# The scan of a two-block kernel: its small triangular solve on POOL, one scaling on ACT, and another order of the work in each step

## The chip, the cores and the metric

The kernel runs on one core of one Trainium2 chip. The metric is the device time of one execution in microseconds. The engines are PE (TensorE: matrix products), DVE (VectorE: elementwise work), ACT (ScalarE: functions and copies), POOL (GpSimd) and SP, which here only issues DMAs. Each takes its own queue in order; they wait for each other by semaphores.

## The reference

Two model blocks run one after the other on 512 tokens of width 1024, with 256 context tokens beside them. The first block has two layers. Each layer projects the tokens, runs a convolution over half of the channels and a recurrent scan over the other half, and then a gated feed-forward network. The second block has attention, retention and a mixture of 32 experts. The change touches the recurrent scan of the first block alone:

```python
def step(s, inp):                       # s: state, 64 x 64 for each of 8 heads
    r_t, k_t, v_t, w_t, kk_t, b_t = inp
    sa = -einsum("bhvk,bhk->bhv", s, kk_t)
    s = s * w_t[:, :, None, :] + sa[..., None] * b_t[:, :, None, :] + v_t[..., None] * k_t[:, :, None, :]
    y = einsum("bhvk,bhk->bhv", s, r_t) if emit else None
    return s, y
```

It runs forwards and backwards over the tokens, first over the 256 context tokens and then, from the state reached there, over the 512 tokens of x, in each of the two layers. Everything is float32.

## The kernel before

The scan of a layer is cut into 12 steps: four pairs of heads (a pair fills the 128 partitions), and for each pair three groups of 256 tokens. A step handles one group forwards and one backwards (the two entries of T), each as four chunks of 64 tokens. Within a chunk the recurrence becomes matrix products of 64x64 with the inverse of a triangular matrix I + N, which does not depend on the state. So for each step s these pieces of work are prepared ahead of the chunks:

- decays(s): the decay factors of all tokens (L842 to L876), with a memset on POOL at L860. Its two buffers tA and tB come from a ring of four, so that one step's decays can live at a time.
- products(s) (L878 to L913): scaled keys and queries (L886 to L892, on DVE), and their products on PE (L904), masked on DVE into GM (L908). One part of GM is N. For every third step norm_kk (L725) normalises the keys of a new pair first, through a buffer that the finish of an earlier pair also uses.
- solve(s) (L674 to L695): the inverse of the 16x16 blocks on the diagonal of I + N. N goes out to DRAM with four DMAs on SP (L682), and comes back as NB with one block to each of 64 partitions (L684). There 14 steps of substitution run, each one multiplication (L689) and one addition (L690) with k rows of 15 - k elements; the diagonal is set at L693, and the result goes out to DRAM (L694). NB is one buffer, the products' DRAM copies are two in turn.
- inverse(s): four DMAs on SP bring the blocks' inverses back in the layout of N (L702, in solved). DVE transposes them (L948), and by products on PE with copies on ACT and DVE between them (L954 to L1003) the 16x16 blocks grow to the whole 64x64 inverse XI. Beside it the keys are transposed on PE (L924).
- chunks(s) (L1009 to L1065): for each of four chunks the chain psR (PE, L1021 and L1024), rg (DVE, L1027), psS (PE, L1031), Z (ACT, L1033), psM (PE, L1039) and the new state M (DVE, L1044). M[:, 1] is the old state scaled by the decay of the chunk; L1043 writes it on POOL, and L1044 adds the new part.

The order is written out by generators. `abreast` takes one yield of each generator in turn; `among` runs the chunks of step s as the main work of 25 positions and spreads over them 16 yields of `to_come(s)` and 14 of `others(s)` (convolution taps at L533, gates of later layers with their weight loads at L250, the finish of an earlier pair). `to_come(s)` takes three yields of the inverse of s + 1 and then the rest of it abreast with products, solve and the following decays of s + 2. The Tile framework then plans the order on every engine from this: an instruction that comes earlier as written has priority, and one that its cost model takes to be ready may be moved ahead of one that is not.

Of the kernel before, what the change touches and what calls it, by code (L numbers as in the profile page):

```python
# [16 lines left out]
AF = mybir.ActivationFunctionType  # L17
OP = mybir.AluOpType
# [110 lines left out]
def tile_two_blocks(ctx: ExitStack, tc: tile.TileContext, I: dict, out: bass.AP, dump=None, stop=None):  # L129
    nc = tc.nc  # L130
# [51 lines left out]
    ones = const.tile([128, 128], F32, name="ones")  # L182
# [491 lines left out]
    def solve(s, T, gs):  # L674

        for q, (d, _) in zip(T, gs):
            src = q["NT"]
            if d:
                src = wk.tile([128, 4, 64], F32, name="Nt", tag="ar", bufs=1)
                nc.vector.transpose(src, q["NT"])  # L680
            for h in range(2):
                nc.sync.dma_start(own(NSC[s % 2], d, h), src[HR[h]])  # L682
        NB = wk.tile([64, 16, 16], F32, name="NB", tag="nb", bufs=1)
        nc.sync.dma_start(NB, blocks(NSC[s % 2]))  # L684
        yield
        for k in range(1, 15):
            t = wk.tile([64, 64], F32, name="nbt", tag="nbt", bufs=1)[:, 0:k * (15 - k)].rearrange("p (a b) -> p a b", a=k)
            sh = [64, k, 15 - k]
            nc.vector.tensor_tensor(t, NB[:, 0:k, k:k + 1].to_broadcast(sh), NB[:, k:k + 1, k + 1:16].to_broadcast(sh), op=OP.mult)  # L689
            nc.vector.tensor_tensor(NB[:, 0:k, k + 1:16], NB[:, 0:k, k + 1:16], t, op=OP.add)  # L690
            if k % 2:
                yield
        nc.vector.tensor_scalar(NB.rearrange("p a b -> p (a b)")[:, 0:256:17], ones[0:64, 0:16], 1.0, None, op0=OP.mult)  # L693
        nc.sync.dma_start(blocks(XSC[s % 2]), NB)  # L694
        yield  # L695

# [7 lines left out]
    def scan(l, S):  # L704
        RK, VY, WA = S["RK"], S["VY"], S["WA"]
        xd = dr.tile([128, KT * TT], F32, name=f"xd{l}")
        nc.sync.dma_start(xd, XT.rearrange("p a b -> p (a b)"))

        rkd = dr.tile([128, 2, 2, TT], F32, name=f"rkd{l}")
        wr = (TX if l == 1 else TT, TT)  # L710
        for i, w in enumerate(wr):
            nc.sync.dma_start(rkd[:, i, :, 0:w], RK[:, i, 2:4, 0:w])
        get = scan_buffers(l == 0, RK)
        w = TT if l == 0 else TX

        mods = [(0, u) for u in range(4, 12)] if l == 0 else []
        ZZ = [wk.tile([128, TT], F32, name=f"zz{i}", tag="z", bufs=zb[0]) for i in range(3)]
        S["rs"], S["V"] = ZZ[2], {}
        KKs, Ts, states = {}, {}, [[None, None] for _ in range(4)]

        def norm_kk(pr):

            KK = ZZ[pr % 2]
            for (a, n), p in zip(SEG, spread_halves(S["RN"][:, pr], 6, "pp", ZZ[2])):
                nc.vector.scalar_tensor_tensor(KK[:, a:a + n], RK[:, 1, pr % 2, a:a + n], vc("k_k", 4 * l + pr), p, op0=OP.mult, op1=OP.mult)  # L725
            KKs[pr] = KK

        def parts(s):
            pr, step = s // 3, s % 3
            return pr, step, [(0, step), (1, (0, 2, 1)[step])], not (l == 1 and step == 0)  # L730

        def decays(s):
            pr, step, gs, emit = parts(s)
            Ts[s] = [{}, {}]
            yield from abreast(decay(q, l, S, pr, d, g) for q, (d, g) in zip(Ts[s], gs))

        def every(f, s):
            pr, step, gs, emit = parts(s)
            yield from abreast(f(q, l, S, pr, d, g, KKs[pr], get, emit) for q, (d, g) in zip(Ts[s], gs))

        def blocks_of(s):
            if s % 3 == 0:
                norm_kk(s // 3)
                yield
            yield from every(products, s)
            yield from solve(s, Ts[s], parts(s)[2])

        def inverse_of(s):
            solved(s, Ts[s], parts(s)[2], get)
            yield from every(transposed, s)  # L750
            yield from inverse(Ts[s], parts(s)[2])

        def blocks_then_decays(s):
            yield from blocks_of(s)
            if s + 1 < 12:
                yield from decays(s + 1)

        def to_come(s):

            works = []  # L760
            if s + 1 < 12:
                works.append(inverse_of(s + 1))
                for _ in range(3):
                    yield next(works[0])
            if s + 2 < 12:
                works.append(blocks_then_decays(s + 2))
            yield from abreast(works)

        wcs = {}

        def conv_out(m):

            if m % 2 == 0 or not wcs:
                wcs[m // 2] = load_w(I["w_out"][l], 0, 4, (m // 2) * 256, 256)
            o = XT[:, m]
            if m < AHEAD_M:
                o = wk.tile([128, TT], F32, name="xm", tag="acc", bufs=1)
                nc.sync.dma_start(o[:, 0:w], xd[:, m * TT:m * TT + w])
            for i, (a, n) in enumerate(SEG[:1] if l == 1 else SEG):
                p = bank("pg", None, "pco")  # L780
                for kt in range(4):
                    nc.tensor.matmul(p[:, 0:n], lhsT=wcs[m // 2][:, kt, m % 2 * 128:m % 2 * 128 + 128], rhs=S["CV"][kt][:, a:a + n], start=kt == 0, stop=kt == 3)
                yield
                gated(o[:, a:a + n], p[:, 0:n], S["MOD"][:, i, 16 + m:17 + m], l == 1 and a < TX)
            if m < AHEAD_M:
                nc.sync.dma_start(xd[:, m * TT:m * TT + w], o[:, 0:w])
            yield

        def others(s):
            for f in S["conv"].get(s, ()):  # L790
                yield from f(S["rs"]) or ()
                yield
            for i, u in mods[s * len(mods) // ADA_STEPS:(s + 1) * len(mods) // ADA_STEPS]:
                ada(i, u)
                yield
            if s >= CONV_OUT:
                for m in range((s - CONV_OUT) * AHEAD_M // (12 - CONV_OUT), (s + 1 - CONV_OUT) * AHEAD_M // (12 - CONV_OUT)):
                    yield from conv_out(m)
            if s % 3 == 0 and s:
                yield from finish(l, S, s // 3 - 1)  # L800
                if s // 3 < 3:
                    for i, w in enumerate(wr):
                        nc.gpsimd.dma_start(RK[:, i, s // 3 - 1, 0:w], rkd[:, i, s // 3 - 1, 0:w])


        run(decays(0))
        run(blocks_of(0))
        run(decays(1))
        run(inverse_of(0))
        run(blocks_of(1))  # L810
        run(decays(2))
        for s in range(12):
            pr, step, gs, emit = parts(s)
            among(chunks(l, S, pr, gs, Ts[s], states[pr], emit, step == 2, get), MAIN, (to_come(s), AHEAD), (others(s), OTHERS[s]))
        for m in (*range(AHEAD_M, KT), *range(AHEAD_M)):
            nc.sync.dma_start(XT[:, m, 0:w], xd[:, m * TT:m * TT + w])
        run(abreast([finish(l, S, 3), chain(*(conv_out(m) for m in range(AHEAD_M, KT)))]))
# [7 lines left out]
    def run(work):  # L825
        for _ in work:
            pass
# [181 lines left out]
    def chunks(l, S, pr, gs, T, state, emit, final, get):  # L1009
# [4 lines left out]
        def chunk(q, d, n):  # L1014
            po = py[:, d] if emit else None
            c = n if d == 0 else 3 - n
            KR, GM, Z, BT, XI, PC = (q[k] for k in ("KR", "GM", "Z", "BT", "XI", "PC"))
            M = state[d]
# [16 lines left out]
            if not (final and n == 3):  # L1035
                pm = bank("sm", None, "psM")
                for i in range(2):
                    for h in range(2):
                        nc.tensor.matmul(pm[HR[h], 0:64], lhsT=BT[HR[h], c, i], rhs=Z[i][HR[h], c], start=i == 0, stop=i == 1)  # L1039
                yield  # L1040
                Mn = get("Mn").rearrange("p (a v) -> p a v", a=2)
                if M is not None:
                    nc.gpsimd.tensor_scalar(M[:, 1], M[:, 0], PC[:, c:c + 1], None, op0=OP.mult)  # L1043
                    nc.vector.scalar_tensor_tensor(Mn[:, 0], pm[:, 0:64], PC[:, c:c + 1], M[:, 1], op0=OP.mult, op1=OP.add)  # L1044
                else:
                    nc.vector.tensor_scalar(Mn[:, 0], pm[:, 0:64], PC[:, c:c + 1], None, op0=OP.mult)
                state[d] = Mn
# [310 lines left out]
    for t in range(6):  # L1358
        p = bank("pre", None, "rvt")
# [63 lines left out]
    for t in range(4):  # L1423
        for a, n in SEG:
            p = bank("pre", None, "pq")
# [8 lines left out]
    p = bank("w", None, "ppe")  # L1434
# [9 lines left out]
    for t in range(6):  # L1444
        r = LAT[:, 4 + t:5 + t]
        for i in range(2):
            p = bank("pre", None, "pkv")
# [19 lines left out]
    for t in range(6):  # L1467
        rk = SS[:, 4 + t]
        k, kp = KTL[t], KP[:, t:t + 1]
# [747 lines left out]
```

## Time and profile before

| | us |
|---|---|
| median of three runs | 4015.07 (4010.14 to 4015.51) |
| the profiled execution | 4013.53 |
| its span, first to last instruction | 4011.7 |
| PE busy in the span | 3774.9 |
| DVE busy | 2731.7 |
| ACT busy | 1695.0 |
| POOL busy | 333.9 |
| L689 and L690 together, DVE | 125.3 |
| L1043, POOL | 84.8 |

A stretch of the profile is read as the busy time of each engine in it; where two engines work at once, both are counted. In the lists of groups a row has the line, the engine, the operation, what it writes and reads by the program's names, its shape and its count, then its busy time and the mean duration of one, and then how long the engine stood idle just before such instructions, and for whom. A tile of the scan's buffers is shown as XT or scanbuf, since these buffers are cut from them. Starts are microseconds from the first instruction. The first scan lies at 289 to 691 us, the second at 1519 to 1869 us.

### The profile page before, as it was taken

The numbers are of one execution on the slowest core, as the hardware profiler recorded it, in microseconds if no ns is written. First come the engines' busy times: TensorE is split into PE (matmuls) and PEld (weight loads), VectorE is DVE, ScalarE is ACT, GpSimd is POOL, SyncE is SP. The second block draws the span as 40 slices with busy tenths as digits, with TensorE's granted clock in tenths as the row PEclk, the third lists the DMA queues.
The fourth block names the chain that finished last, engine by engine and source line by source line (L and its number), as shares of the span: only waits on it lengthen the run. The fifth ranks groups of instructions, "written<-read, shape, count | busy, mean of one in ns | idle before, by whom it ended". The sixth has DMA issues, their size and how long they took to land. (4 is left out here: it accounts for less than half of the span.)

```text
span 4011.7 us, 69029 instructions
## 1 busy us (share of the span) xinstructions
PE 3774.9 (94%) x27579; PEld 2827.9 (70%) x27579; DVE 2731.7 (68%) x5439; ACT 1695.0 (42%) x2530; POOL 333.9 (8%) x349
## 2 busy tenths in 40 slices
PE   6998999999999998999999998996999999999997
PEld 4787777888888786776787786675565777664443
DVE  4779865843433778876744545657877899987776
ACT  3233342321212334452322334544655677666555
POOL 0001111000000001110000000001101122122111
PEclk7999999999999998899999998997999999999999
DMA  6122323332322321124445421035979899998996
GB/s 204 47 79 69 115 71 98 117 123 84 126 84 85 100 72 25 32 45 125 152 151 153 106 74 42 1 117 198 360 279 351 306 363 363 371 354 331 374 368 240
DMA packets 353911, 677.75 MB, mean 169 GB/s; under 512 B 118759, under 2 KB 230194, under 8 KB 323474
## 3 DMA queue, kind: packets, MB, share of 16 engines
q1 hardware_dynamic: 343024, 636.89, 45.3%
q0 software_dynamic: 9312, 34.56, 3.4%
q8 instruction: 218, 3.57, 0.4%
q10 hardware_dynamic: 1250, 1.85, 0.1%
q14 instruction: 107, 0.88, 0.1%
HBM read 635.33 MB, written 37.90 MB: 168 GB/s over the span
## 5 line engine op out<-in xcount | busy, mean ns | idle before, releaser
L431 ACT ACTIVATE wh<-wst 128x1024 fp32r<-128x1024 f32 (+2 forms) x222 | 222.7, 1004 | 990.7 <-PE pc L441 513.1
L1830 DVE TENSOR_TENSOR ml<-E,mh 128x2048 fp32r<-128x2048 f32 x236 | 536.2, 2286 | 91.5 <-PE pu L1878 44.3
L1829 ACT ACTIVATE mh<-E 128x2048 fp32r<-128x2048 f32 x236 | 447.6, 1916 | 185.9 <-PE pu L1878 146.8
L441 PE MATMUL px<-Hh,wl 128*128 128x512 f32 (+2 forms) x1216 | 487.8, 402 | 13.8 <-DVE wl L432 13.8
L441 PE MATMUL px<-Hh,wh 128*128 128x512 f32 (+3 forms) x1216 | 486.1, 401 | 13.3 <-ACT wh L431 7.1
L441 PE MATMUL px<-Hl,wh 128*128 128x512 f32 (+3 forms) x1216 | 485.5, 400 | 0.6 <-DVE Hl L419 0.6
L432 DVE TENSOR_TENSOR wl<-wst,wh 128x1024 fp32r<-128x1024 f32 (+2 forms) x222 | 255.4, 1151 | 270.6 <-ACT wh L431 268.4
L1878 PE MATMUL pu<-ml,ch 128*64 128x512 f32 (+2 forms) x968 | 272.3, 399 | 22.4 <-DVE ml L1830 22.2
L1878 PE MATMUL pu<-mh,ch 128*128 128x512 f32 (+1 forms) x968 | 279.3, 403 | 6.9 <-DVE ch L1866 4.2
L441 PEld LDWEIGHTS px<-Hh,wh 128*128 128x128 f32 (+1 forms) x1216 | 232.2, 191 | 72.6 <-ACT wh L431 9.4
L441 PEld LDWEIGHTS px<-Hh,wl 128*128 128x128 f32 (+1 forms) x1216 | 231.8, 191 | 72.8 <-DVE wl L432 18.7
L441 PEld LDWEIGHTS px<-Hl,wh 128*128 128x128 f32 (+1 forms) x1216 | 232.4, 191 | 55.6 <-DVE Hl L419 3.5
L533 DVE SCALAR_TENSOR_TENSOR acc<-ZC,VT,acc 128x272 f32<-128x272 f32 (+2 forms) x600 | 253.0, 477 | 2.5 <-ACT acc L528 2.5
L1878 PEld LDWEIGHTS pu<-mh,ch 128*128 128x128 f32 (+1 forms) x968 | 171.8, 184 | 86.5 <-issue 25.0
L1830 DVE TENSOR_TENSOR ml<-st,mh 128x2048 fp32r<-128x2048 f32 x86 | 196.0, 2286 | 42.8 <-PE pu L1878 24.5
L1878 PEld LDWEIGHTS pu<-ml,ch 128*64 128x64 f32 (+2 forms) x968 | 149.4, 159 | 92.0 <-DVE ml L1830 34.1
L441 PE MATMUL pc<-Hh,wh 128*128 128x256 f32 x672 | 193.0, 288 | 1.0 <-ACT Hh L418 0.9
L441 PE MATMUL pc<-Hl,wh 128*128 128x256 f32 x672 | 191.9, 286 | 0.5 <-DVE Hl L419 0.5
L441 PE MATMUL pc<-Hh,wl 128*128 128x256 f32 (+1 forms) x672 | 190.3, 284 | 0.1
L1829 ACT ACTIVATE mh<-st 128x2048 fp32r<-128x2048 f32 x86 | 163.2, 1917 | 55.3 <-PE pu L1878 31.7
L315 DVE SCALAR_TENSOR_TENSOR as<-adt,CS,as 128x512 f32<-128x512 f32 x224 | 161.3, 747 | 36.4 <-DMA adt<-in_w_ada_dram 20.4
L1134 DVE SCALAR_TENSOR_TENSOR XT<-px,MOD,XT 128x512 f32<-128x512 f32 x66 | 49.4, 749 | 188.0 <-PE px L441 187.7
(602 smaller groups left out, 7864.2 us busy)
## 6 DMA issues: line engine op xcount, KB each, us to landing
E<-in_w_mlp_dram SPq DMA_DIRECT2D x288, 1024.0 KB
st<-in_w_mlp_dram SPq DMA_DIRECT2D x94, 1024.0 KB
wst<-in_w_in_dram SPq DMA_DIRECT2D x29, 1024.0 KB
adt<-in_ada_w_dram SPq DMA_DIRECT2D x96, 256.0 KB
adt<-in_w_ada_dram SPq DMA_DIRECT2D x96, 256.0 KB
wst<-in_ffn_wg_dram SPq DMA_DIRECT2D x22, 1024.0 KB
wst<-in_ffn_wu_dram SPq DMA_DIRECT2D x22, 1024.0 KB
adaw<-in_ada_w_dram SPq DMA_DIRECT2D x16, 1024.0 KB
```

Of the source, the lines that this page charges most:

```text
L315: nc.vector.scalar_tensor_tensor(acc[s], t, c, acc[s], op0=OP.mult, op1=OP.add)
L431: nc.scalar.activation(wh, t[:, :, c0:c0 + n], AF.Copy)
L432: nc.vector.tensor_tensor(wl, t[:, :, c0:c0 + n], f32(wh), op=OP.subtract)
L441: nc.tensor.matmul(p[0:m, 0:n], lhsT=wa[:, k, 0:m], rhs=ha[:, k, a:a + n], start=k == 0 and first, stop=k == nk - 1 and last)
L533: nc.vector.scalar_tensor_tensor(o, z[:, j + a:j + a + n], cw(j), o, op0=OP.mult, op1=OP.add)
L1134: nc.vector.scalar_tensor_tensor(o, src, gate, o, op0=OP.mult, op1=OP.add)
L1829: nc.scalar.activation(wh, t, AF.Copy)
L1830: nc.vector.tensor_tensor(wl, t, f32(wh), op=OP.subtract)
L1878: nc.tensor.matmul(p[0:xa.shape[2]], lhsT=xa[:, kt], rhs=w[part][:, c:c + 512], start=kt == 0 and j == 0, stop=last and j == len(parts) - 1)
```

## The change

The substitution of the solve is issued to POOL in place of DVE, with the diagonal. The scaling of the old state M goes from POOL to ACT. The old blocks_of is cut into products_of and solve_of. In `to_come(s)` the products of step s + 2 now stand first; then the solve of s + 2, followed by the decays of s + 3, runs abreast with the inverse of s + 1, the solve's generator first. Ahead of the steps, the products of step 1 are written before the inverse of step 0, and its solve behind it.

```diff
--- before.py
+++ after.py
@@ -686,11 +686,11 @@
         for k in range(1, 15):
             t = wk.tile([64, 64], F32, name="nbt", tag="nbt", bufs=1)[:, 0:k * (15 - k)].rearrange("p (a b) -> p a b", a=k)
             sh = [64, k, 15 - k]
-            nc.vector.tensor_tensor(t, NB[:, 0:k, k:k + 1].to_broadcast(sh), NB[:, k:k + 1, k + 1:16].to_broadcast(sh), op=OP.mult)
-            nc.vector.tensor_tensor(NB[:, 0:k, k + 1:16], NB[:, 0:k, k + 1:16], t, op=OP.add)
+            nc.gpsimd.tensor_tensor(t, NB[:, 0:k, k:k + 1].to_broadcast(sh), NB[:, k:k + 1, k + 1:16].to_broadcast(sh), op=OP.mult)
+            nc.gpsimd.tensor_tensor(NB[:, 0:k, k + 1:16], NB[:, 0:k, k + 1:16], t, op=OP.add)
             if k % 2:
                 yield
-        nc.vector.tensor_scalar(NB.rearrange("p a b -> p (a b)")[:, 0:256:17], ones[0:64, 0:16], 1.0, None, op0=OP.mult)
+        nc.gpsimd.tensor_scalar(NB.rearrange("p a b -> p (a b)")[:, 0:256:17], ones[0:64, 0:16], 1.0, None, op0=OP.mult)
         nc.sync.dma_start(blocks(XSC[s % 2]), NB)
         yield
 
@@ -738,11 +738,13 @@
             pr, step, gs, emit = parts(s)
             yield from abreast(f(q, l, S, pr, d, g, KKs[pr], get, emit) for q, (d, g) in zip(Ts[s], gs))
 
-        def blocks_of(s):
+        def products_of(s):
             if s % 3 == 0:
                 norm_kk(s // 3)
                 yield
             yield from every(products, s)
+
+        def solve_of(s):
             yield from solve(s, Ts[s], parts(s)[2])
 
         def inverse_of(s):
@@ -750,20 +752,20 @@
             yield from every(transposed, s)
             yield from inverse(Ts[s], parts(s)[2])
 
-        def blocks_then_decays(s):
-            yield from blocks_of(s)
+        def solve_then_decays(s):
+            yield from solve_of(s)
             if s + 1 < 12:
                 yield from decays(s + 1)
 
         def to_come(s):
 
+            if s + 2 < 12:
+                yield from products_of(s + 2)
             works = []
+            if s + 2 < 12:
+                works.append(solve_then_decays(s + 2))
             if s + 1 < 12:
                 works.append(inverse_of(s + 1))
-                for _ in range(3):
-                    yield next(works[0])
-            if s + 2 < 12:
-                works.append(blocks_then_decays(s + 2))
             yield from abreast(works)
 
         wcs = {}
@@ -804,10 +806,12 @@
 
 
         run(decays(0))
-        run(blocks_of(0))
+        run(products_of(0))
+        run(solve_of(0))
         run(decays(1))
+        run(products_of(1))
         run(inverse_of(0))
-        run(blocks_of(1))
+        run(solve_of(1))
         run(decays(2))
         for s in range(12):
             pr, step, gs, emit = parts(s)
@@ -1040,7 +1044,7 @@
                 yield
                 Mn = get("Mn").rearrange("p (a v) -> p a v", a=2)
                 if M is not None:
-                    nc.gpsimd.tensor_scalar(M[:, 1], M[:, 0], PC[:, c:c + 1], None, op0=OP.mult)
+                    nc.scalar.activation(M[:, 1], M[:, 0], AF.Copy, scale=PC[:, c:c + 1])
                     nc.vector.scalar_tensor_tensor(Mn[:, 0], pm[:, 0:64], PC[:, c:c + 1], M[:, 1], op0=OP.mult, op1=OP.add)
                 else:
                     nc.vector.tensor_scalar(Mn[:, 0], pm[:, 0:64], PC[:, c:c + 1], None, op0=OP.mult)
```

## Rows read from the trace of the kernel before

**Rows 1.** The page, part 1: busy us, share of the span, instructions of each engine

```profile
PE 3774.9 (94%) x27579; PEld 2827.9 (70%) x27579; DVE 2731.7 (68%) x5439; ACT 1695.0 (42%) x2530; POOL 333.9 (8%) x349
```

**Rows 2.** Busy time by stretch: its length, then PE, PEld, DVE, ACT, POOL busy (count)

```profile
345.00:500.00 155.00, 145.54 (x2886) 115.32 (x2886) 135.12 (x502) 56.39 (x158) 25.52 (x50) 0.97 0.38 110
500.00:691.00 191.00, 182.32 (x3301) 140.30 (x3300) 118.81 (x436) 73.65 (x186) 22.00 (x52) 0.98 0.30 77
1568.00:1700.00 132.00, 122.42 (x2530) 103.00 (x2532) 111.39 (x430) 51.01 (x146) 24.62 (x50) 0.87 0.16 31
1700.00:1869.00 169.00, 157.72 (x3023) 122.13 (x3020) 109.70 (x414) 72.41 (x184) 21.12 (x50) 0.96 0.26 62
```

**Rows 3.** Groups of instructions by line on DVE, whole span

```profile
L689 DVE TENSOR_TENSOR nbt<-NB 64x14 f32<-64x14 f32 (+6 forms) x336 | 62.8, 187 | 6.1 <-DMA NB<-nsc 3.2
...
L690 DVE TENSOR_TENSOR NB<-NB,nbt 64x14 f32<-64x14 f32 (+6 forms) x336 | 62.5, 186 | 2.5
```

**Rows 4.** DVE in order of time: first and last operations of solves

```profile
313.30 0.15 DVE L689 TENSOR_TENSOR nbt<-NB 64x14 f32<-64x14 f32 x1
...
328.01 0.17 DVE L690 TENSOR_TENSOR NB<-NB,nbt 64x14 f32<-64x14 f32 x1
...
642.02 0.17 DVE L689 TENSOR_TENSOR nbt<-NB 64x14 f32<-64x14 f32 x1
...
1537.58 0.16 DVE L689 TENSOR_TENSOR nbt<-NB 64x14 f32<-64x14 f32 x1
...
1628.27 0.16 DVE L689 TENSOR_TENSOR nbt<-NB 64x14 f32<-64x14 f32 x1
...
1773.12 0.16 DVE L689 TENSOR_TENSOR nbt<-NB 64x14 f32<-64x14 f32 x1
...
1828.92 0.16 DVE L689 TENSOR_TENSOR nbt<-NB 64x14 f32<-64x14 f32 x1
...
1836.28 0.18 DVE L690 TENSOR_TENSOR NB<-NB,nbt 64x14 f32<-64x14 f32 x1
```

**Rows 5.** SP in order of time: a tight turn, scan 2, steps 3 to 4

```profile
1618.69 0.57 SPq L694 DMA_DIRECT2D xsc<-NB  x1
1621.22 2.61 SPq L702 DMA_DIRECT2D XT<-xsc  x4
1623.93 0.57 SPq L684 DMA_DIRECT2D NB<-nsc  x1
```

**Rows 6.** SP in order of time: a late turn, scan 2, steps 8 to 9

```profile
1753.53 0.59 SPq L694 DMA_DIRECT2D xsc<-NB  x1
...
1764.28 1.38 SPq L682 DMA_DIRECT2D nsc<-scanbuf  x2
...
1769.31 0.59 SPq L684 DMA_DIRECT2D NB<-nsc  x1
```

**Rows 7.** Groups on POOL by line and shape, whole span

```profile
L1791 POOL TENSOR_TENSOR hr<-hr,AS 128x512 f32<-128x512 f32 x8 | 12.8, 1607 | 5.8 <-DVE hr L1790 2.9 <-DVE AS L1780 2.8
...
L1043 POOL TENSOR_SCALAR XT<-XT,PC 128x64 f32<-128x64 f32 x160 | 84.8, 540 | 453.8 <-DVE XT L1044 281.6 <-DVE NB L690 120.9 <-DVE nbt L689 40.4
...
L860 POOL MEMSET tA<- 128x4 f32 x48 | 4.6, 105 | 682.3 <-PE pc L441 254.0 <-DVE acc L533 253.6 <-DVE nbt L689 54.8
```

**Rows 8.** Line 1043: duration ns min/median/max, first and last start

```profile
L1043 POOL TENSOR_SCALAR XT<-XT,PC x160: 434/446/2484, 347.3 to 1864.2; 128x64 f32<-128x64 f32 x160
```

**Rows 9.** Groups on ACT and DVE, 345 to 691 us

```profile
L1033 ACT ACTIVATE scanbuf<-psS 128x64 f32<-128x64 f32 x96 | 18.4, 223 | 85.9 <-PE psS L1031 85.8
...
L1044 DVE SCALAR_TENSOR_TENSOR XT<-psM,PC,XT 128x64 f32<-128x64 f32 x80 | 21.1, 276 | 18.5 <-PE psM L1039 18.1 <-POOL XT L1043 0.2
```

**Rows 10.** DVE and POOL in order of time, second block

```profile
2732.94 0.74 DVE L1790 SCALAR_TENSOR_TENSOR hr<-xr,RS,AS 128x512 f32<-128x512 f32 x1
...
2733.81 1.76 DVE L1790 SCALAR_TENSOR_TENSOR hr<-xr,RS,AS 128x512 f32<-128x512 f32 x1
...
2733.76 1.26 POOL L1791 TENSOR_TENSOR hr<-hr,AS 128x512 f32<-128x512 f32 x1 [1.50 <-DVE hr L1790]
```

## The prediction

> **What bounds the kernel now.** I read the page first: PE is busy for 94% of the span and DVE for 68%, POOL for 8% [rows 1]. The change touches the two scans alone, so the next view is the busy time of each engine in four stretches of them [rows 2]. In the first half of each scan DVE is busy 135.1 of 155 us and 111.4 of 132 us; in the second half 118.8 of 191 and 109.7 of 169. POOL has 22 to 26 us of work in each. PE reads 94% there too, but these are thousands of 64x64 products whose modelled ends overlap, and it waits inside its queue for the other engines; I do not take it for the bound.
>
> The third view is the order of time. The solve (L689, L690) is a chain of 28 small operations, each needing the last. Its buffer NB exists once, so solve s+1 can load only after solve s has been written out. I read its start and end in all 24 steps; the first and the last stand in [rows 4]. First start to last start is 313.30 to 642.02 us in the first scan, 11 intervals of 29.9 us, and 1537.58 to 1828.92 in the second, 11 of 26.5 us. A solve takes 14.9 us in the first step (313.30 to 328.18) and 7.5 in the last; the mean of 24 is 13.3 us. The scan steps at the solve's pace: an interval is one solve plus a turn of 13 to 17 us. On SP the turn has two forms. In a tight one [rows 5] the products of the next step are already written: the result goes out at 1618.69, the four loads of the inverse start at 1621.22 and take 2.6 us, then NB is loaded at 1623.93, and the next solve starts at 1628.27 [rows 4]. In a late one [rows 6] the result goes out at 1753.53, but the next products are first written out at 1764.28, NB is loaded at 1769.31 and the solve starts at 1773.12 [rows 4]. Counting by whether the products' first write is issued before or after the result of the solve ahead, 13 of the 22 intervals are tight and 9 late, the late ones nearly all in the second halves.
>
> **The change part by part.**
>
> *Solve on POOL.* 24 times 28 operations and a diagonal write leave DVE: 62.8 + 62.5 = 125.3 us [rows 3], 5.2 us a step. They come to POOL, where no row shows a two-input operation this small (14 to 56 elements on 64 partitions). Bounds from POOL's own rows: from below 0.105 us, a memset of 4 elements; from above 1.607, a two-input operation on 512 elements [rows 7]. The nearest row is L1043, one input, 64 elements: 0.540 mean, with a minimum of 0.434 and a median of 0.446 [rows 7, 8]. I take 0.54, since the mean holds the waits that POOL already has beside DVE, and the second input and the smaller size roughly offset each other. 29 x 0.54 = 15.7 us, against 13.3: +2.4 us a solve. At 0.105 it would be 3 us, and then the chunks and the inverse would bound; at 1.607 it would be 47. The L860 memset (0.105) and the loads of L803 queue behind the solve on POOL; they are for a step later, and hidden.
>
> *DVE without the solve.* In a late interval the next products share DVE with the running solve. Of the 5.2 us that leave I give half, 2.6 us, to the products' chain, because the other half lay in DVE's waits; bounds 0 and 5.2. In a tight interval this gains nothing, since the products wait there already.
>
> *Products first.* In the order as written they come behind three yields of the inverse; now they stand at the head of the step. A step's work is spread over 25 positions of the chunks, so 3/25 of the mean interval of 28 us = 3.4 us earlier, in late intervals alone. Bounds 0 (the planner had moved them up already) and the 10.8 us between 1753.53 and 1764.28 [rows 6].
>
> *Solve's transfers ahead of the inverse's.* The NB load of s+2 is now written ahead of the four loads of the inverse of s+1 on SP. Both are released by the same transfer. In tight intervals NB is loaded 2.7 us earlier (1621.22 to 1623.93, [rows 5]); the inverse pays one issue of 0.6 us, which is not in the chain of the solves. Where the planner still puts the products' writes there and they are late, SP, which takes its queue in order, holds up the inverse.
>
> *Scaling of M on ACT.* 160 operations leave POOL and come to ACT. The nearest ACT row is L1033, 128x64: 0.223 us [rows 9], about 36 us in both scans, where ACT is busy 253 of 647 us [rows 2]. M is scaled while the chunk goes through psR, rg, psS and Z, and needed only at L1044, whose wait for POOL was 0.2 us in the first scan [rows 9]. What covers it is that chain; without the cover 0.22 us for each chunk would come on, 0.9 us a step for four chunks, and below nothing POOL's 0.54 us comes off. I take 0. Queued behind it on ACT is the copy L1033 of the same chunk.
>
> Sum: late 9 x (2.4 - 2.6 - 3.4) = -32; tight 13 x (2.4 - 2.7) = -4; the two first solves, before which no chain runs, 2 x 2.4 = +5. In all -31 us. The profiled execution took 4013.5 us (span 4011.7), so 3982.5; the median of the runs shown is 1.5 above that execution, which gives **3984 us**.
>
> **A rule against it.** While a POOL operation with two inputs on 512 elements runs (1.26 us at 2733.76), the DVE operation L1790 beside it takes 1.76 us, where the one just before took 0.74 [rows 10]: DVE was held for 1.0 us. In the other direction L1043 goes from 0.434 up to 2.484 us [rows 8]. The Trainium skill, "GPSIMD Engine Reference", sections 1 and 8, says that POOL shares its interfaces to SBUF with VectorE and contends with DVE instructions that have two SBUF inputs or run in a 2-port mode; section 4.1 advises against elementwise work on POOL, about 2x slower with two inputs. The trace agrees on the first. By the factor 2 alone an operation would cost 2 x 0.187 = 0.37 us as an estimate, and the solve would be shorter than now, with a sum of about -150 us; the first rule is the second rival below.
>
> **The rivals.**
>
> 1. *POOL's price is the new bound.* The sum has its break-even where the solve is 3.7 us longer than now (24 x 3.7 = 89 = 13 x 2.7 + 9 x 6.0), at 17.0 us, or 0.59 us an operation. That is only 9% above my price. For it: the solve's operations have two inputs, and each waits for the last, which the pairs of L1043 do not. At 0.65 us the solve takes 18.9 us, +5.5: 13 x 2.8 - 9 x 0.5 + 2 x 5.5 = +43, 4058 us. Against: L1043 alone needs 0.446.
>
> 2. *DVE pays back by being held.* The same place, another price: each of 672 POOL operations holds a DVE operation. Held for 1.0 us at 512 elements, 40 elements (the mean of k(15-k) over 14) would scale to 0.08 us, 54 us of DVE in all, less than half of what leaves. It decides from 125/672 = 0.19 us on. Held for a whole POOL operation of 0.45 us, DVE loses 302 and gains 125; if a third of the difference reaches the end, as in a DVE about 75% busy, +59: 4074 us.
>
> 3. *Nothing comes of it.* Late turns are set by something else: the normalisation of k that waits for the finish of an earlier pair, or a load queued on SP. Then only the solve's +2.4 and the -2.7 are left, between -8 and +8: 4007 to 4023 us.
>
> **How the numbers follow.** Within 0.2%, about 8 us, a measurement of this kernel cannot tell a gain from none. Forecast with its neighbours on the fast side (0.30 to 0.57 us an operation) 0.54, its own range 3930 to 4006; the third rival 0.13; the first 0.23 and the second 0.10. So faster 0.54, same 0.13, slower 0.33. The range runs from 3930, where the interval falls by 3.5 us in 24 steps and the products of PE no longer hide behind the solve, to 4075, where 0.66 us an operation or the second rival lead; about 0.1 is left out on either side.
>
> **What would show it.** POOL's rows of the solve give the price at once: below 0.59 us the chain is not longer in sum. Right if the start-to-start of the solves falls from 29.9 and 26.5 us to about 28 and 25.5, if the late intervals go from 9 to a few, and if NB's load stands ahead of the inverse's four on SP. DVE's busy time must fall by about 125 us; if it falls by less than 70, or the means of L533 and L889 rise, the second rival is at work. If L1044 waits for ACT, the scaling was not hidden. Wrong altogether if the solves take 13 to 16 us on POOL and the interval stays where it is: then the solve never set the pace.

## The result, and the profile after

The changed kernel takes 4047.88 us in the median (4042.55 to 4049.18), the kernel before beside it 4015.29. The ratio is 1.0087, with a 95% interval of 1.0069 to 1.0105: slower by 33 us, where 31 us faster was forecast. The time lies within the stated range, on its other side.

The first row of the page, and the busy times of the four stretches that answer to [rows 2] (length, then PE, PEld, DVE, ACT, POOL busy, granted clock, DMA share, GB/s):

```profile
PE 3781.0 (93%) x27579; PEld 2843.2 (70%) x27579; DVE 2654.9 (66%) x4743; ACT 1735.7 (43%) x2688; POOL 461.7 (11%) x885
```

```profile
345.00:525.00 180.00, 160.96 (x2903) 126.65 (x2900) 120.45 (x344) 69.58 (x195) 46.70 (x158) 0.88 0.34 96
525.00:712.00 187.00, 173.86 (x3258) 135.82 (x3257) 100.80 (x289) 82.78 (x224) 47.93 (x155) 0.97 0.29 77
1588.00:1730.00 142.00, 121.85 (x2694) 103.79 (x2690) 103.95 (x298) 69.90 (x203) 50.53 (x169) 0.93 0.17 33
1730.00:1902.00 172.00, 156.72 (x2978) 123.96 (x2978) 88.95 (x259) 78.46 (x221) 43.22 (x153) 0.92 0.24 59
```

The loss lies in the scans. These are the same busy times from the first decay scan to the last chunk of each scan, of the kernel before and then of the changed one:

```profile
289.60:690.70 401.10, 367.36 (x6751) 288.24 (x6751) 307.21 (x1099) 155.78 (x401) 49.03 (x109) 0.96 0.31 85
1519.40:1868.70 349.30, 314.87 (x6094) 253.22 (x6094) 260.61 (x972) 148.47 (x389) 46.36 (x106) 0.90 0.21 45
```

```profile
289.90:711.60 421.70, 373.41 (x6751) 295.27 (x6751) 270.18 (x751) 178.23 (x481) 115.50 (x377) 0.92 0.30 81
1541.40:1901.50 360.10, 308.05 (x6093) 252.61 (x6094) 220.73 (x624) 166.21 (x467) 108.21 (x374) 0.89 0.20 44
```

The two scans went from 750.4 to 781.8 us, 31.4 of the 34.3 us by which the span grew. PE is busy as long as before (682.2 and 681.5 us, though the granted clock fell from 0.96 and 0.90 to 0.92 and 0.89), DVE 76.9 us less. ACT and POOL got more work, but are idle for more than half of the scans: it is waiting that grew.

POOL's price is the opposite of what was feared [rows 4, 7]. The solve's groups on POOL, and the first and last operations of one solve in order of time:

```profile
L690 POOL TENSOR_TENSOR NB<-NB,nbt 64x14 f32<-64x14 f32 (+6 forms) x336 | 105.5, 314 | 24.2
L689 POOL TENSOR_TENSOR nbt<-NB 64x14 f32<-64x14 f32 (+6 forms) x336 | 103.0, 307 | 321.4 <-DMA NB<-nsc 297.2
```

```profile
1600.23 0.20 POOL L689 TENSOR_TENSOR nbt<-NB 64x14 f32<-64x14 f32 x1 [8.57 <-DMA NB<-nsc]
...
1610.44 0.33 POOL L690 TENSOR_TENSOR NB<-NB,nbt 64x14 f32<-64x14 f32 x1
```

One operation takes 0.31 us, a whole solve 11.1 us in the mean of 24, 2.2 us less than on DVE, where it was interleaved with other work. POOL stands idle for 321.4 us in all before L689, 297.2 of them until NB is loaded: the solver waits for its input. The starts of the solves lie 31.1 and 26.6 us apart (before 29.9 and 26.5), the first Z copies of the chunks (L1037, before L1033) 32.2 and 27.2 us (before 30.1 and 26.1). A turn has grown from 16.1 and 12.9 us to 19.7 and 15.5. On SP the late form of [rows 6] is now the rule, 18 of 22 intervals where it was 9:

```profile
1748.54 0.59 SPq L694 DMA_DIRECT2D xsc<-NB  x1
1751.08 2.56 SPq L702 DMA_DIRECT2D XT<-xsc  x4
1755.27 1.25 SPq L682 DMA_DIRECT2D nsc<-scanbuf  x2
1760.08 1.24 SPq L682 DMA_DIRECT2D nsc<-Nt  x2
1763.35 0.59 SPq L684 DMA_DIRECT2D NB<-nsc  x1
```

Where the waiting starts is seen in one stretch of all engines (start, duration, engine, in brackets the idle time before and what ended it):

```profile
1858.02 0.46 DVE L1031 TENSOR_SCALAR rg<-psR 128x64 f32<-128x64 f32 x2 [0.32 <-PE psR L1028]
...
1862.55 0.22 POOL L690 TENSOR_TENSOR NB<-NB,nbt 64x14 f32<-64x14 f32 x1
1862.79 0.57 SPq L694 DMA_DIRECT2D xsc<-NB  x1
...
1864.17 0.68 PE L1043 MATMUL psM<-scanbuf 64*64 64x64 f32 x16
...
1865.33 2.60 SPq L702 DMA_DIRECT2D XT<-xsc  x4
1868.43 0.45 DVE L952 STREAM_TRANSPOSE XT<-XT 128x256 f32<-128x256 f32 x1 [9.96 <-DMA XT<-xsc]
1869.68 0.45 DVE L952 STREAM_TRANSPOSE XT<-XT 128x256 f32<-128x256 f32 x1 [0.80 <-DMA XT<-xsc]
...
1870.68 0.46 DVE L1048 SCALAR_TENSOR_TENSOR XT<-psM,PC,XT 128x64 f32<-128x64 f32 x2
...
1871.00 0.48 PE L1025 MATMUL psR<-scanbuf,scanbuf 64*64 64x64 f32 x4 [5.57 <-DVE XT L1048]
```

Read it from below: PE waits 5.57 us for the next state M (L1048). M stands on DVE behind the first transposes of the next step's inverse (L952), and these hold DVE idle for 9.96 us, because the solve on POOL ends only at 1862.77, and its result needs a trip through DRAM. What M itself needs from PE, psM (L1043), was there at 1864.85. The planner put the transposes ahead of M, where they can't run yet.

Such a wait may have a second price. PE's granted clock in this wait and just behind it (columns as in the stretches above):

```profile
1865.40:1870.00 4.60, 0.03 (x1) 0.00 (x0) 0.77 (x2) 0.00 (x0) 0.00 (x0) 0.99 0.25 57
1870.00:1876.80 6.80, 5.80 (x108) 5.80 (x110) 3.07 (x10) 1.59 (x6) 0.00 (x0) 0.50 0.24 80
```

PE had stood idle, and then the clock was at 0.50 (1.2 GHz in place of 2.4) for 6.8 us. In the changed kernel 257 of the inverse's 768 left products (L958) started at this level, before 50; one takes 311 ns there and 219 at 2.4 GHz, in the median. How much of the loss this is, no run holds apart.

The row of the transposes (busy, mean ns, idle just before) is the one to compare. The kernel before, with the left products that follow on PE, and the changed kernel:

```profile
L948 DVE STREAM_TRANSPOSE XT<-XT 128x256 f32<-128x256 f32 x48 | 21.0, 437 | 9.1 <-DMA XT<-xsc 8.9
L954 PE MATMUL py<-XT,scanbuf 64*64 64x64 f32 x768 | 36.1, 228 | 9.1 <-DVE XT L948 7.6 <-DMA XT<-xsc 1.4
```

```profile
L952 DVE STREAM_TRANSPOSE XT<-XT 128x256 f32<-128x256 f32 x48 | 20.9, 440 | 77.2 <-DMA XT<-xsc 77.0
```

DVE stands 77 us in front of them, where it stood 9.

### The profile page after: what moved, and what is told of

Same layout as the page of the kernel before. It is cut to its first block, busy times and chain, and to the rows that moved or that the text cites. A ratio compares the mean times of both kernels' runs of the same rounds, so it can differ in the third digit from the quotient of the medians.

```text
span 4046.0 us, 68992 instructions
## 1 busy us (share of the span) xinstructions
PE 3781.0 (93%) x27579; PEld 2843.2 (70%) x27579; DVE 2654.9 (66%) x4743; ACT 1735.7 (43%) x2688; POOL 461.7 (11%) x885
## 5 line engine op out<-in xcount | busy, mean ns | idle before, releaser
L441 PE MATMUL px<-Hh,wh 128*128 128x512 f32 (+3 forms) x1216 | 484.0, 400 | 13.6 <-ACT wh L431 7.1
L441 PEld LDWEIGHTS px<-Hh,wl 128*128 128x128 f32 (+1 forms) x1216 | 230.7, 190 | 72.8 <-DVE wl L432 19.7
L533 DVE SCALAR_TENSOR_TENSOR acc<-ZC,VT,acc 128x272 f32<-128x272 f32 (+2 forms) x600 | 251.2, 482 | 2.5 <-ACT acc L528 2.5
L1833 ACT ACTIVATE mh<-st 128x2048 fp32r<-128x2048 f32 x86 | 163.3, 1918 | 54.3 <-PE pu L1882 31.2
L315 DVE SCALAR_TENSOR_TENSOR as<-adt,CS,as 128x512 f32<-128x512 f32 x224 | 161.5, 749 | 37.6 <-DMA adt<-in_w_ada_dram 20.9
L1961 POOL DMA_INDIRECT out_dram<-XT,idx x34 | 116.2, 3417 | 512.7 <-DVE XT L1959 284.3
```

The source lines that it names most:

```text
L315: nc.vector.scalar_tensor_tensor(acc[s], t, c, acc[s], op0=OP.mult, op1=OP.add)
L441: nc.tensor.matmul(p[0:m, 0:n], lhsT=wa[:, k, 0:m], rhs=ha[:, k, a:a + n], start=k == 0 and first, stop=k == nk - 1 and last)
L533: nc.vector.scalar_tensor_tensor(o, z[:, j + a:j + a + n], cw(j), o, op0=OP.mult, op1=OP.add)
L1833: nc.scalar.activation(wh, t, AF.Copy)
L1961: nc.gpsimd.indirect_dma_start(out=ov, out_offset=bass.IndirectOffsetOnAxis(ap=idx[:, 0:1], axis=0), in_=y, in_offset=None, compute_op=OP.add)
```

## The experiments

Ratios are to the kernel before, timed beside each group of runs (its medians there were 4005 to 4009 us), with 95% intervals. Where microseconds are said to go by the ratios, they are a ratio, or a difference of two, times 4007 us. The place of the inverse is the share of the chunks of step s (by psS) that stand ahead of the first left product of step s + 1 in PE's queue, mean over the steps: 0.74 before, 0.41 changed.

**e1 to e4: which part costs.** The changed kernel with solve and scaling put back (order alone); the kernel before with one or both of the other edits.

```diff
-            nc.vector.tensor_tensor(t, NB[...
+            nc.gpsimd.tensor_tensor(t, NB[...            # e2, e4
-                    nc.gpsimd.tensor_scalar(M[:, 1], ...
+                    nc.scalar.activation(M[:, 1], ...    # e3, e4
```

> The new order of the work alone; the solve stays on DVE and the scaling of M on POOL. Theory A (the order costs: products now stand ahead of the inverse, whose last stage is put behind all chunks of the step ahead in 21 of 24 steps, as against 15 before): slower than the kernel before, by 15 to 40 us, 4030 to 4055, with the inverse of a step taking 12 us or more from first transpose to last copy. Theory B (the solve on POOL costs, by its price or by holding DVE; the order is harmless): within 10 us of the kernel before. Theory C (the scaling on ACT costs): the same as the kernel before.

> The solve on POOL alone; order and scaling as before. Theory A: faster than before, since the solve takes 11 us in place of 13 and in the planned order the inverse now ends ahead of the last chunk of the step ahead in 21 of 24 steps: the gap between the chunks of two steps falls from 11 us to 4 to 7 us, 22 gaps, so 30 to 120 us less, 3895 to 3985. Theory B: slower by 25 us or more, 4040 or above. Theory C: about the kernel before or faster.

> The scaling of M on ACT alone; solve on DVE, order as before. Theories A and B: within 8 us of the kernel before, 4007 to 4023. Theory C: slower by 20 us or more.

> Solve on POOL and scaling on ACT, with the order as before. Theory A: as fast as the solve on POOL alone, within 10 us of it. Theory B: slower than the kernel before, 4040 or above. Theory C: slower than the solve on POOL alone by 20 us or more.

Measured: e1 3992.08 us, 0.9955 [0.9938, 0.9972]; e2 4126.61, 1.0304 [1.0278, 1.0331]; e3 4007.12, 1.0004 [0.9988, 1.0021]; e4 4115.67, 1.0254 [1.0209, 1.03]. The order gains 0.45%, the scaling on ACT is free, and the solve on POOL costs 3% in the old order. In e2 a solve takes 11.8 us against 13.3, so it isn't POOL's price for the solve. The same two rows in e2 say where to look; its inverse stands at 0.28, and 684 of its 768 left products ran at 1.2 GHz:

```profile
L948 DVE STREAM_TRANSPOSE XT<-XT 128x256 f32<-128x256 f32 x48 | 21.2, 443 | 135.2 <-DMA XT<-xsc 135.0
L954 PE MATMUL py<-XT,scanbuf 64*64 64x64 f32 x768 | 52.0, 304 | 105.7 <-DVE XT L948 101.6 <-DVE rg L1027 4.0
```

**e5 to e7: the place of the inverse.** Edges of order, which put an instruction behind another in its own engine's queue and add no wait between engines. e5 is the kernel before with the inverse early (n counts the four chunks of a step from 0); e6 is e2 and e7 the changed kernel, with the inverse late. In e6 and e7 the whole inverse, its loads on SP with it, is also written out later.

```diff
+            with behind(n, 1, "left"), behind(n, 3, "right2"):      # e5, psS; rg of n = 1 behind "first"
                 nc.tensor.matmul(ps_[HR[h], 0:64], ...
...
+            while s and len(MARK[s - 1]) < 5: yield                 # e6, e7, in inverse_of(s)
+            with tc.issue_after(m): each(f)                         # first: fifth rg, left: fifth psS
```

> The kernel before, its solve on DVE. One thing is added: edges of order (no waits of their own) that set the inverse of s + 1 into the queues where the kernel with the solve alone on POOL has it: on DVE its first transposes, and on PE its first left products (L954), stand ahead of the second of the four pairs of chunks of step s (place 0.25, where the kernel before has 0.74 in the mean), and the last products of L993 ahead of the fourth. Theory D (the place costs: the order planned with the solve on POOL puts the inverse ahead of chunks whose turn it blocks while it waits for the load xi): time rises by most of the +120 us of solve-on-POOL alone, to 4070-4150, scan intervals of 31 to 35 us, and waits of PE and DVE of 50 us a scan at L954 and L948. Rival B2 (POOL's operations hold DVE): no operation is on POOL that was not, 4000-4030.

> The kernel with the solve alone on POOL (4127 us), in the order of before as written, with edges of order that keep the inverse of s + 1 behind the first five of the eight chunks of step s: its first transposes on DVE behind the fifth rg, its left products on PE behind the fifth psS (place 0.79 in the mean; before 0.74; solve-on-POOL alone 0.28). Theory D: back to the kernel before or below it, 3960-4020, with intervals of 24 to 29 us and DVE busy about 50 us under before. Rival B2 (POOL's 672 operations hold DVE): POOL has the same work beside DVE, so it stays above 4080.

> The changed kernel (4048 us) with the same edges of order: inverse of s + 1 behind the first five chunks of step s (place 0.90 in the mean; the changed kernel 0.41). Theory D: the changed kernel's loss is this place, so it falls below the order-only kernel with the solve on DVE (3992): 3940-3990. Rival B2: 4030-4060, as without the edges. A third result, 3992 to 4020, would say that the place was the loss, and that the solve on POOL brings nothing even without it.

Measured: e5 4028.89, 1.005 [1.0035, 1.0065]; e6 4040.15, 1.0082 [1.0057, 1.0108]; e7 4026.58, 1.0044 [1.0031, 1.0057]. Each moved the way theory D says, and none by all of it. By the ratios e6 gives back 89 of e2's 122 us and e7 17 of the changed kernel's 35. Early, the solve on DVE loses 20 us, not 120: the place alone doesn't make the loss. There DVE stands only 17.5 us in front of the transposes. A likely reason, not tried apart, is that the solve is in the same queue, ahead of them. In e6 the row is at 41:

```profile
L952 DVE STREAM_TRANSPOSE XT<-XT 128x256 f32<-128x256 f32 x48 | 20.3, 433 | 41.4 <-DMA XT<-xsc 41.2 <-issue 0.2
```

**DVE held by POOL, from the same traces.** In the changed kernel's scans I compared each DVE line's operations that POOL's solve covers by at least 40% with those that it doesn't touch. Most of those with all operands in SBUF are longer beside it (L891 415 to 467 ns, L893 683 to 726, L533 479 to 494, the small copy L899 162 to 211), but not the transposes (L982 302 and 296); those that read PSUM are not (L1031 218 and 218, L1048 277 and 276). All of it sums to some 8 us, in e2 to some 11. The rival is real and small.

**e8: a second NB.** Order-only, with solve s + 1 in the other 64 partitions.

```diff
+        hf = HR[s % 2]
-        NB = wk.tile([64, 16, 16], F32, name="NB", tag="nb", bufs=1)
+        NB = S["NB"][hf]
```

> The order-only kernel (3992 us: the new order, the solve on DVE, the scaling on POOL) with NB and nbt twice, in partitions 0 to 63 and 64 to 127 in turn, so that the load of solve s + 1 need not wait until solve s is written out. If the solve with its turn sets the pace, as the prediction said: the turn loses the 2.5 us of the result's transfer and up to 5 us with the load, 22 x 2 to 4 us: 3900-3950. If it doesn't set the pace (theory D: the inverse and chunks on PE and DVE do): 3975-4000.

Measured: 4046.91, 1.0091 [1.0062, 1.0121], 55 us slower than e1, which neither theory has. Taking the wait for NB away didn't shorten the steps (30.8 and 26.6 us against 29.1 and 24.4); a solve took 15.2 us in place of 13.0, and DVE stood no longer before the transposes (4.8 us, in e1 9.7). Why it is slower stays open.

**e9 to e12: what bounds the scan, and the wait itself.**

```diff
+                    nc.tensor.matmul(po[HR[h], c], lhsT=Z[1][HR[h], c], rhs=GM[HR[h], 1, c, 1], start=True, stop=True)   # e9, alone
-  ... own(XSC[s % 2], d, h))
+  ... own(XZ, d, h))                                                # e10
+            if 1 < k < 14: (yield as before); continue              # e11
```

> The kernel before, with four of the six products that make y in each chunk left out (the two of L1051, and those of L1054 with i = 0; y lacks these terms): 1248 of PE's 12845 matmuls in the two scans, at 52 to 54 ns each by PE's busy time in them (682.2 us), about 65 us. They stand on no chain towards the next state, and nothing on DVE, ACT or POOL goes away. Theory P (PE's work and PE's waits add up to the scans' time; PE is the bound that the prediction dismissed): 45 to 85 us less, 3925 to 3965. Rival, the prediction's reading (the chain of solves sets the pace, PE only looks busy): nothing, 3995 to 4020.

> The changed kernel, where the four loads of the inverse read a DRAM copy of zeros in place of the solve's result (the diagonal blocks of the inverse are zero): the same solve on POOL and the same instructions everywhere, but no inverse waits for a solve. Theory D with P (PE and DVE stand at the head of their queues for the transfer of the solve's result, and PE's waits are the loss): PE's waits at the left products, psR and psS in the scans, 57 us in the changed kernel and 15 in order-only, fall by 20 to 45 us, and the time from 4048 to 4000-4030. Rival (POOL's operations cost in another way, by holding DVE or by what queues behind them): 4035 to 4055.

> The kernel before with only the first and the last of the 14 substitution steps of the solve (on DVE; the blocks' inverses lack the rest): 24 of its 28 operations go, 24 x 24 x 0.187 = 107 us of DVE, and 10 us or more of each solve. The prediction's reading (an interval is one solve plus its turn, so the scan steps at the solve's pace): 22 intervals lose up to 10 us each, 3780 to 3870. Theory P: only PE's waits can go, 64 us in both scans, about 30 of them where a scan starts: 3955 to 4000.

> The changed kernel with the solve back on DVE: the new order and the scaling on ACT. If the solve on POOL is all of the loss, it stands where order-only stood, 3980 to 4002, and the solve on POOL costs about 55 us in the new order. Rival: the scaling on ACT (0.34 us there, 55 us of ACT in all, ahead of copies of chunks in its queue) costs beside the new order, though it cost nothing in the old: 4015 to 4048.

Measured: e9 3996.94, 0.9968 [0.9953, 0.9982]; e10 3979.27, 0.9931 [0.9907, 0.9955]; e11 3950.19, 0.9848 [0.9828, 0.9869]; e12 3995.94, 0.9965 [0.9949, 0.9981].

Theory P falls with e9: 1248 matmuls less gave 10 us (13 by the ratio). The busy row of PE shows why (its two scans):

```profile
287.40:691.60 404.20, 365.24 (x6034) 276.39 (x6032) 310.21 (x1100) 155.25 (x401) 49.18 (x109) 0.92 0.31 85
1515.30:1856.60 341.30, 303.82 (x5597) 233.65 (x5598) 262.19 (x973) 145.08 (x388) 47.91 (x106) 0.92 0.21 48
```

669.1 us in place of 682.2, 10 ns for each matmul that went, not 52: busy PE contains waiting, as the prediction held. e11 strikes the prediction's own reading: the solve shrank from 13.6 and 13.1 us to 1.9 and 1.4, and the chunks' interval only from 30.1 and 26.1 to 29.2 and 24.6. These are the first Z copies of each scan's first and last step, 11 intervals apart, before and then in e11:

```profile
345.47 0.36 ACT L1033 ACTIVATE scanbuf<-psS 128x64 f32<-128x64 f32 x2
...
676.08 0.34 ACT L1033 ACTIVATE scanbuf<-psS 128x64 f32<-128x64 f32 x2 [4.57 <-PE psS L1031]
...
1568.07 0.36 ACT L1033 ACTIVATE scanbuf<-psS 128x64 f32<-128x64 f32 x2
...
1855.53 0.34 ACT L1033 ACTIVATE scanbuf<-psS 128x64 f32<-128x64 f32 x2 [2.85 <-PE psS L1031]
```

```profile
332.35 0.34 ACT L1037 ACTIVATE scanbuf<-psS 128x64 f32<-128x64 f32 x2
...
653.31 0.34 ACT L1037 ACTIVATE scanbuf<-psS 128x64 f32<-128x64 f32 x2 [4.57 <-PE psS L1035]
...
1534.41 0.34 ACT L1037 ACTIVATE scanbuf<-psS 128x64 f32<-128x64 f32 x2
...
1805.49 0.34 ACT L1037 ACTIVATE scanbuf<-psS 128x64 f32<-128x64 f32 x2 [2.84 <-PE psS L1035]
```

The planner moved the inverse in e11 too, to 0.27. In e5 such a place cost 20 us, 0.9 us an interval, so it hides little of the 11.7 us that each solve lost. Of e11's 56 us (61 by the ratio), 24 come before the first chunks of the two scans (55.8 to 42.5 us and 48.7 to 37.6), where the solve is on the path, and some 26 (11 x 0.9 + 11 x 1.5) from the 22 intervals. In e10 the inverse loads zeros and waits for no solve, with POOL's solve unchanged and the inverse in about the same place (0.38). 62 us go by the ratios. 31 of them lie before the first chunks, where the kernel before waits for a solve as well; what bears on the loss are the 28 us in the intervals (32.2 and 27.2 to 31.2 and 25.7), of the 36 us that these had lost. DVE still stands 37.8 us before the transposes there, for the loads of the zeros. e12 fixes the price of POOL's solve in the new order at 49 us by the ratios (1.0087 to 0.9965).

**e13 to e15: the decays earlier.** In e6 the products of a step started 12 us behind the chunks whose buffers they take (from the last Z copy of step s - 3 to the first scaled key of step s), before 7; on DVE the decays ahead of them stood later in the queue.

```diff
-            yield from solve_of(s)
-            if s + 1 < 12:
-                yield from decays(s + 1)
+            yield from abreast([solve_of(s)] + ([decays(s + 1)] if s + 1 < 12 else []))
```

> e6_late_on_pool (4040 us: before's order, the solve on POOL, the inverse behind five chunks), with one edit to the order as written: decays(s + 1) runs abreast with the solve of s in place of behind it. Theory D2: what was left of the loss in e6 are the decays, which with the solve on POOL stand 0.18 steps (about 5 us) later among the chunks on DVE (scan L866 at 1.01 steps behind the start of step s - 3, before 0.83), so that the first operation of the products starts 12 us behind the end of chunks s - 3 in place of 7: that gap goes back to 7 us or less, 4040 to 3985-4015. Rival Q (POOL's solve costs by itself, by its semaphores or by what its operations do to others): stays at 4030-4045.

> e7_changed_late (4027 us: the changed kernel, the inverse behind five chunks) with the same edit: decays abreast with the solve. The changed kernel's decays stand at 0.85 to 0.90 steps, order-and-ACT's at 0.79; with the edit 0.38. Theory D2: 3975 to 4005, level with the order-and-ACT kernel (3996), since then all that the order of POOL's solve costs is gone. Rival Q: 4015 to 4030.

> Control: e12_order_and_act (3996 us, solve on DVE) with the same edit, decays at 0.36 steps. If the edit only mends what POOL's solve does to the order, it does nothing here: 3988 to 4004. If earlier decays are worth as much with the solve on DVE, 3960 to 3985, and then e13 and e14 say nothing on POOL alone.

Measured: e13 4031.1, 1.005 [1.0031, 1.007]; e14 4015.46, 1.0017 [1.0004, 1.003]; e15 3990.49, 0.9961 [0.9944, 0.9978]. The gap closed (from 12 to 5.5 us in e13, from e7's 5.5 to 2.6 in e14), and 11 to 13 us came back by the ratios with the solve on POOL, none that can be told with it on DVE. Less than D2 had, and the gap isn't the reason by itself: the changed kernel and e12 both have 5.1 us, and e15 closed it to 1.2 for nothing.

**e16 to e18: the products' transfers out of SP's queue.** SP's own waits (us in total, times, longest) in the second scan, before and changed:

```profile
SPq L694 <- DVE NB L690: 22.3, 2, 12.3
```

```profile
SPq L694 <- POOL NB L690: 99.2, 10, 12.8
```

With the solve on POOL, SP stands in front of the result's write 10 times for the end of the solve, and what is queued behind it are the next products' writes. Before, other operations of DVE's queue are often named as the releaser; SP's waits in front of L694 for all causes are 72 us there and 146 us changed.

```diff
-                nc.sync.dma_start(own(NSC[s % 2], d, h), src[HR[h]])
+                nc.gpsimd.dma_start(own(NSC[s % 2], d, h), src[HR[h]])
-        nc.sync.dma_start(NB, blocks(NSC[s % 2]))
+        nc.gpsimd.dma_start(NB, blocks(NSC[s % 2]))
-        nc.gpsimd.memset(full[:, 0, :, 0:1], 0.0)
+        nc.vector.memset(full[:, 0, :, 0:1], 0.0)
```

> e14_changed_late_decays (4015 us: the solve on POOL, new order, inverse late, decays early) with the four writes of the products' N (L682) and the load of NB (L684) issued by POOL, and the memset of the decays on DVE so that it doesn't queue behind them. SP keeps the result's write L694 and the inverse's loads L702. Theory S: what is left of the loss is SP's queue, where in 9 or 10 of 11 intervals of a scan the next products' writes stand behind L694 and L702, which wait for the solve (before: 4 or 5); the time from the products to their last write falls from 5 us to 2, the turn by 3 to 6 us, and the time to 3980-4000. Rival Q (POOL's operations cost by themselves) or a slow issue on POOL: 4010 to 4040.

> Control: e15_order_act_decays (3990 us, solve on DVE) with the same two edits (writes of N and load of NB from POOL, memset on DVE). If the queue is what POOL's solve made bad, nothing here: 3982 to 4000. If a free queue helps either solve: 3960 to 3980, the best so far. If issuing from POOL is dear: above 4000.

> The changed kernel (4048 us) with the same two edits alone, the inverse and the decays left where the changed kernel has them. Theory S with D: the two losses add up, so that this gives back the queue's part, 10 to 25 us, 4022 to 4038, and the inverse's part stays. If SP's queue is no cause: 4040 to 4060.

Measured: e16 3995.55, 0.9975 [0.9966, 0.9985]; e17 3997.49, 0.9983 [0.9973, 0.9994]; e18 4044.17, 1.0104 [1.0087, 1.0121]. e16 gains 17 us on e14 by the ratios and is level with its control e17, which lacks the edges: with inverse, decays and transfers out of each other's way, the solve on POOL costs nothing that can be told, and gains nothing. The row of the transposes in e14, and in e16:

```profile
L954 DVE STREAM_TRANSPOSE XT<-XT 128x256 f32<-128x256 f32 x48 | 20.2, 431 | 26.8 <-DMA XT<-xsc 26.4 <-issue 0.2
```

```profile
L954 DVE STREAM_TRANSPOSE XT<-XT 128x256 f32<-128x256 f32 x48 | 20.0, 429 | 19.0 <-DMA XT<-xsc 19.0
```

e18 missed: without the late inverse the same edits give nothing (the row is at 90 us there). So the parts don't add up: the transfers show only beside the other two edits, and the early decays weren't tried without the late inverse. Over e14, e16 holds two edits (the transfers, and the memset on DVE), and how they share the gain wasn't tried apart.

By the ratios, in steps from the changed kernel to e16: late inverse -0.43%, early decays -0.27%, own queue -0.42%; in all 1.12 of the 1.22% between the changed kernel and e12. These are steps in this order, not shares that stand by themselves. Of the kernels that leave nothing out the quickest are e1, e15 and e12, 0.9955 to 0.9965, which their intervals don't tell apart. They beat both kernels, with the solve on DVE.

## Why the prediction was wrong

- *"The scan steps at the solve's pace"* is the step that failed. It was read from 24 starts and ends of solves, but that the solve fills half of an interval doesn't make it the limit: e11 took 11.7 us from each solve, and an interval lost 0.9 and 1.5 us. All three terms of the sum hang on that step, and so does rival 1's break-even. In the changed kernel the time went where the solve's result was waited for, in queues taken in order (e6, e7, e10, e16), and not into its length.
- *The price, 0.54 us an operation*, was too high. An operation takes 0.31 us, and a solve of 29 takes 11.1 us, so 0.38 from start to start. The step failed by its size; even with the right price (-2.2 us a solve in place of +2.4) the sum would have come out at -142 us, further off. The Trainium skill, "GPSIMD Engine Reference", section 4.1, put two-input work on POOL at about twice DVE's time; the trace has 314 to 186 ns, a factor of 1.7.
- *DVE without the solve, 2.6 us in a late interval*: DVE's busy time fell by 76.8 us, not by 125. That is no sign of rival 2: neighbours overlap much of the solve, and taken out of the trace before, its operations leave DVE's busy time only 56 us shorter. Summed one by one, DVE's operations fell by 115 us where 129 left, so the others grew by 14. The prediction's other sign rose a little: L533 from 477 to 482 ns, L889 (L893 in the changed kernel) from 680 to 699.
- *Products first, and NB's load ahead of the inverse's*: late intervals went from 9 to 18, not to a few, and NB's load stood ahead of the four loads once in 22. The planner reordered what the order as written had moved. Even so the new order alone gains (e1), with 4 such loads and 10 late intervals: 18 us by the ratio, where the two terms had 9 x 3.4 + 13 x 2.7 = 66.
- *Scaling on ACT at nothing* was right (e3, e12), though one costs 0.34 us, not 0.22.
- *Rival 1* (POOL's price) is out by the price, *rival 2* (DVE held) by its size of some 8 us, *rival 3* held the mildest form of the truth, that late turns are set elsewhere. What happened was in none. The solve's move changed where the planner put the inverse, the decays and the transfers in queues that are taken in order, and DVE, PE and SP stood at the head of them for a result that wasn't there.
- *The PE row* was read rightly as no bound, as far as e9's matmuls off the chain show it.

What sets the steady interval of 25 to 30 us is open. Neither less PE work (e9) nor a shorter solve with 576 operations less on DVE (e11) moved it much. The products of step s start 7 us in the mean behind the last chunk of step s - 3, whose buffers they take; a longer ring wasn't tried. Nor was the wait that rival 3 named: the gap is widest at the first steps of the third and the fourth pair (19.9 and 19.4 us, 13.0 and 16.2), where norm_kk comes first.

## What to carry to other kernels

Before moving work to another engine, ask what the planner will do with the time that it believes is gained: an instruction that waits for the moved chain may be put ahead of work that is ready, and in a queue taken in order that can cost more than the chain did (e2 lost 122 us; a solve cut almost away, in e11, gave 61). Look for one row whose idle time is put down to a transfer (here the first transposes of the inverse, 9 us before and 77 after) and put that instruction late with an edge of order. That an operation recurs at the kernel's period doesn't show that it sets the period: shorten it, and look.

## What was not expected of the hardware

- Small two-input operations on POOL (14 to 56 elements on 64 partitions) took 0.31 us in the mean (0.20 with 14 elements where nothing held them up, by the first row of that solve), less than the 0.446 us of a one-input operation with 64 elements on 128 partitions [rows 8].
- Most DVE operations beside them were longer if all their operands lay in SBUF: 3% at L533, 13% at L891, 30% at L899, whose copies take only 0.16 us otherwise. Transposes in SBUF (L982) and operations that read PSUM (L1031, L1048) were no longer.
- 1248 of the scans' 12845 matmuls left out shortened them by 4.9 us (750.4 to 745.5), although PE's rows show it busy for 91% of the time.
